# Tying modulation columns behind vector operations, ordering a feed-forward opening further by hand, and copying out one product

## The chip, the cores and the metric

One NeuronCore of a Trainium2 chip runs the whole program in one launch. The metric is the device time of an execution in microseconds (us); lower is better. Matrix products run on TensorE (PE in the profile), elementwise work on VectorE (DVE) and ScalarE (ACT), masks and a few accumulating transfers on GpSimd (POOL), and almost all transfers are issued from SyncE's queue (SP).

## The reference, cut to what matters

The kernel computes one layer of a transformer block for 512 tokens of width 1024 in float32, starting with six modulation vectors from a condition `c`:

```
mod = silu(c) @ w_ada + b_ada                  # 6 vectors of 1024
shift1, scale1, gate1, shift2, scale2, gate2 = split(mod, 6)
h = rmsnorm(x, g1) * (1 + scale1) + shift1
... = split(h @ w_in)                          # two branches' q, k, v, gates
merged = g_sb * (stick_breaking(...) @ w_proj_sb) + g_ret * (retention(...) @ w_proj_ret)
x = x + gate1 * (merged @ w_out)
h = rmsnorm(x, g2) * (1 + scale2) + shift2
a, u = split(h @ w_ffn_in)                     # 2 x 2816 columns
x = x + gate2 * ((silu(a) * u) @ w_ffn_out)
return rmsnorm(x, g_final)
```

Retention has four heads; each normalises its output and multiplies it by `silu(r_g)`.

## The kernel before, in words

Activations lie transposed, eight tiles of 128 features x 512 tokens. Each float32 operand is split into a high and a low part (ScalarE rounds the high part, VectorE subtracts it to give the low part, lines 205 and 207), and a product is three matmuls (line 226 in the profile, through `mm3`): high x high, high x low, low x high. Weights come as 512 KB blocks through three `raw` buffers into four `whi` and four `wlo` tiles. PSUM has eight banks: four named `ps`, three named `z`, one `av`.

Outside of stretches marked `manual_schedule` a planner sets the order of the instructions on every engine: it runs the program against its own model of costs, and takes, of what is ready there, what was written first. Inside such a stretch VectorE, ScalarE and TensorE keep the written order. `tc.issue_after(ins)` puts what is written under it behind `ins` on the engine of `ins`; transfers are not bound by it. Every engine executes its instructions in the fixed order, so one that waits holds all behind it.

**Modulation columns.** A 128-wide piece of `mod` is made on VectorE: a block of `w_ada` is multiplied by the broadcast `silu(c)` and summed along its row (line 254, one instruction and a small read of the sum), and the bias is added (line 257). `ada(n)` makes two such columns and loads two blocks (512 KB each) into the two `araw` buffers. n = 0 to 7 (shift1, scale1) are made in a hand-ordered start. n = 8 to 23 (gate1, shift2, scale2, gate2) are needed only from 740 us on; they are written at the end of each retention head, four per head, and the planner puts them where it sees room.

**Retention.** For each head `ret_scores` multiplies queries and keys (24 matmuls, tiles q), splits the scores (lines 205, 209) and masks them on GpSimd (line 599); `ret_out` multiplies by the values (tiles s, v); `ret_gate` makes four gate products of 24 matmuls, each ending in two multiplications and a split on VectorE (lines 789, 790, 207); then come the next head's queries, keys (rotated on VectorE, lines 680 to 682) and values (split, line 207, tile v); `ret_proj` makes eight projections (line 809 adds them up). The products of the next head begin while the last one's vector work goes on.

**Start.** While the first `x` tiles are squared and summed, `keep_busy(6)` gives TensorE six matmuls that no one reads.

**Feed-forward.** The input product for a pair of 256-column stripes p (11 of them) is a 2 x 2 block scheme of seven products (1 to 7) of sums of weight quarters with sums of activation quarters (S1 to S4, A11 and so on). In stripe p product 5 starts bank `v` and product 3 adds to it; between them the content after product 5 alone is used: line 1095 adds it to the sum u3 once product 7 is there, into the tile of `p1`. The weight sums t5, t6, t7, t4 are made on VectorE (line 1010), from quarters of which two lie in the `araw` buffers. Some low parts are made without VectorE: ScalarE writes the negated high part (line 969) and GpSimd issues a transfer that adds the raw weight onto it (line 970).

**The opening** (lines 1192 to 1302) is ordered by hand from the last output products to stripe 0's products 4, 6, 5, 7. Those are written with `late=True`: high x high and low x high first, and high weight x low activation in a second pass. After them the planner orders stripe 2's product 1, stripe 0's product 3, stripe 2's product 2 and stripe 1's product 6, their operands, and all that follows:

```
    queue = list(work)
    with tc.issue_after(held), tc.issue_after(held_act):
        del queue[:3]
        load_raws(1, [(0, 1), (1, 1)])
        sums(1, t5="s", t6="s", t7="h", t4="h")
```

Here `held` is the low part of S3 on VectorE and `held_act` its high part on ScalarE.

Of the kernel before, what the change touches and what calls it, by code (L numbers as in the profile page):

```python
# [113 lines left out]
def kernel(  # L114
# [9 lines left out]
    nc = tc.nc  # L124
# [78 lines left out]
    def split(dst_hi, dst_lo, src, scale=1.0, eng=None):  # L203

        nc.scalar.activation(dst_hi, src, AF.Copy, scale=scale)  # L205
        if isinstance(scale, float) and scale == 1.0:
            (eng or nc.vector).tensor_sub(dst_lo, src, f(dst_hi))  # L207
        else:
            nc.vector.scalar_tensor_tensor(  # L209
                dst_lo, src, scale, f(dst_hi), op0=ALU.mult, op1=ALU.subtract  # L210
            )
# [13 lines left out]
    def mm(o, lhs, rhs, start, stop):  # L225
        nc.tensor.matmul(o, lhs, rhs, start=start, stop=stop, skip_group_check=True)  # L226
# [208 lines left out]
    with tc.manual_schedule(engines={nc.vector.engine, nc.scalar.engine, nc.tensor.engine}):  # L435
# [23 lines left out]
        keep_busy(6)  # L459
# [320 lines left out]
    def ret_gate(h, os_, y):  # L780
        r = bcast(y, psa())
        ys = []
        for e in range(4):
# [8 lines left out]
            split(hl[:, 0, :], hl[:, 1, :], t)  # L792
            ys.append(hl)
        return ys
# [3 lines left out]
    def ret_proj(h, ys):  # L798
        for i in range(4):
            hi, lo = weight(("pr", h, i))  # L800
            for c in range(2):
# [3 lines left out]
                if p_ret[d] is None:  # L805
                    p_ret[d] = otile()
                    nc.vector.tensor_copy(p_ret[d], o)
                else:
                    nc.vector.tensor_add(p_ret[d], p_ret[d], o)
# [8 lines left out]

    qk = ret_qk(0, qk_ps)
    vt = ret_v(0, v_ps)  # L820
    gains2 = []
    for h in range(RH):
# [181 lines left out]
    def sums(p, **tags):  # L1004
        raw, t = raws_of[p], sums_of.setdefault(p, {})
        for key, tag in tags.items():
# [3 lines left out]
            nc.vector.tensor_sub(t[n], raw[a], t[b] if b in t else raw[b])  # L1010
# [34 lines left out]
    def product(p, n, o, first, last, at=None, then=None, late=False):  # L1045
# [3 lines left out]
        ah, al = acts7[SEVEN[n]]  # L1049
        for i in range(2):  # L1050
            c = slice(i * P, (i + 1) * P)
            for k in range(4):
# [4 lines left out]
                if late:  # L1057
                    mm(oc, hi[:, k, c], ah[:, k, :], a, False)
                    mm(oc, lo[:, k, c], ah[:, k, :], False, False)
                else:  # L1060
                    mm3(oc, hi[:, k, c], lo[:, k, c], ah[:, k, :], al[:, k, :], a, z)
        if late:
            for i in range(2):
                c = slice(i * P, (i + 1) * P)
                for k in range(4):
                    mm(o[:, i * 256 : (i + 1) * 256], hi[:, k, c], al[:, k, :],
                       False, last and i == 1 and k == 3)

    def run_product(p, n):

        d = part.setdefault(p, {})
        if n == 1:
            d["x"] = ps()
            product(p, 1, d["x"], True, False)
            d["p1"] = tmp()
            nc.scalar.activation(d["p1"], d["x"], AF.Copy)
        elif n == 2:
            product(p, 2, d["x"], False, True)
            d["s0"] = tmp()
            nc.scalar.activation(d["s0"], d["x"], AF.Silu)  # L1080
        elif n == 6:
            d["z"] = psz()
            product(p, 6, d["z"], True, True)
            d["u2"] = tmp()
            nc.vector.tensor_add(d["u2"], d["z"], d["p1"])
        elif n == 5:
            d["v"] = psz()
            product(p, 5, d["v"], True, False)
        elif n == 7:
            d["w"] = psz()  # L1090
            product(p, 7, d["w"], True, True)
            d["u3"] = tmp()
            nc.vector.tensor_add(d["u3"], d["w"], d["u2"])
            d["c22"] = d["p1"]
            nc.vector.tensor_add(d["c22"], d["v"], d["u3"])
        elif n == 4:
            d["y"] = ps()
            product(p, 4, d["y"], True, True)
            nc.vector.tensor_add(d["u3"], d["y"], d["u3"])
            nc.scalar.activation(d["u3"], d["u3"], AF.Silu)  # L1100
        else:
            assert n == 3
            product(p, 3, d["v"], False, True)
# [88 lines left out]
    with tc.manual_schedule(engines={nc.vector.engine, nc.scalar.engine, nc.tensor.engine}):  # L1192
# [89 lines left out]
        product(0, 4, d0["y"], True, True, late=True)  # L1282
# [3 lines left out]
        product(0, 6, d0["z"], True, True, late=True)  # L1286
# [4 lines left out]
        held_act = high7("S3", s3, "q")  # L1291
        ready[0, 7] = low(t0[7], k7, wtile("h"))
        held = low7("S3", s3, "q")
# [10 lines left out]
    queue = list(work)  # L1304
    with tc.issue_after(held), tc.issue_after(held_act):
        del queue[:3]
        load_raws(1, [(0, 1), (1, 1)])
        sums(1, t5="s", t6="s", t7="h", t4="h")
        load_raws(2, [(0, 1), (1, 1)])
# [4 lines left out]
    d0["u3"] = tmp()  # L1314
# [144 lines left out]
```

## Time and profile before

| what | value |
|---|---|
| time, median of 3 runs (range) | 1200.77 us (1200.19 to 1202.09) |
| the profiled execution: its own time | 1201.79 us |
| its span, first to last instruction | 1200.0 us |
| TensorE busy | 1173.0 us, 98% |
| VectorE busy | 831.2 us, 69% |
| ScalarE busy | 554.6 us, 46% |
| GpSimd busy | 32.4 us, 3% |
| granted TensorE clock, mean share | 0.995 |

The profiled execution's time is 1.79 us more than its span. The clock share is 1.0 where TensorE was granted its full 2.4 GHz and 0.5 where it was granted 1.2 GHz. Ends of matmuls are modelled, so that TensorE's busy time says little on its pace; idle time and the spacing of starts say more. Stages by time: start to 60 us, retention to about 500, stick-breaking attention to about 750, its projection and the output product to about 830, the opening of the feed-forward to about 875, and the feed-forward to the end.

### The profile page before, as it was taken

What the parts mean: (1) busy time and instruction counts of PE and PEld (TensorE: products, weight loads), DVE (VectorE), ACT (ScalarE), POOL (GpSimd) and SP (SyncE); (2) the same over time, 40 slices, a digit from 0 to 9 for tenths busy, and PEclk for the clock granted to TensorE, in tenths of its full rate; (3) what the DMA queues carried; (4) which work ended last, traced back from release to release, by engine and by line L of the source; (5) the groups of instructions that cost most, each with busy time, mean ns of one, the idle gap of its engine ahead of it and who ended that gap; (6) DMA issues with size and microseconds to landing.
All of it is one profiled execution on the core that took longest, in us unless ns stands there. A gap on an engine that the chain in (4) does not pass through costs nothing.

```text
span 1200.0 us, 16991 instructions
## 1 busy us (share of the span) xinstructions
PE 1173.0 (98%) x6707; PEld 1030.7 (86%) x6707; DVE 831.2 (69%) x1277; ACT 554.6 (46%) x823; POOL 32.4 (3%) x60
## 2 busy tenths in 40 slices
PE   7999899999999999999999999999999999999996
PEld 6988778888888888898889888889999999999996
DVE  7989885545554534377778787756888776767666
ACT  4443323323332332377677778344934544445432
POOL 0010000000000000000000000000100000000000
PEclk9999999999999999999999999999999999999999
DMA  9747771331333255435353635743445654565332
GB/s 351 267 140 229 242 256 59 91 95 47 94 117 88 68 141 152 142 92 127 103 136 98 152 83 161 245 110 86 109 154 163 180 161 112 158 176 158 88 89 71
DMA packets 53136, 167.72 MB, mean 140 GB/s; under 512 B 6592, under 2 KB 8768, under 8 KB 53056
## 3 DMA queue, kind: packets, MB, share of 16 engines
q1 hardware_dynamic: 49168, 154.04, 41.8%
q0 software_dynamic: 3312, 12.06, 5.5%
q8 instruction: 53, 0.87, 0.3%
q10 hardware_dynamic: 576, 0.52, 0.1%
q14 instruction: 27, 0.22, 0.1%
HBM read 135.67 MB, written 4.19 MB: 117 GB/s over the span
## 4 chain that ended last, share of the span: by engine, by line
PE 86%; DVE 6%; DMA 4%; ACT 2%; issue 2%; POOL 0%; SPq 0%; DVEq 0%; POOLq 0%; ACTq 0%
PE ps L226 62%; PE z L226 21%; PE av L226 3%; DMA araw<-wada 3%; DVE araw L254 1%; DVE wlo L207 1%; DMA h<-h 0%; DMA o<-xT 0%; ACT h L1209 0%; DMA t<-t 0%; DVE o L1134 0%; ACT t L626 0%; DVE t L473 0%; DVE s L209 0%; DVE t L682 0%
## 5 line engine op out<-in xcount | busy, mean ns | idle before, releaser
L226 PE MATMUL ps<-h,whi 128*128 128x512 f32 (+1 forms) x1410 | 416.0, 376 | 0.0
L226 PEld LDWEIGHTS ps<-h,whi 128*128 128x128 f32 x1410 | 256.2, 188 | 44.0
L205 ACT ACTIVATE whi<-raw 128x1024 fp32r<-128x1024 f32 (+1 forms) x138 | 144.3, 1046 | 280.1 <-PE ps L226 245.5
L226 PE MATMUL ps<-h,wlo 128*128 128x512 f32 (+1 forms) x705 | 262.6, 376 | 0.0
L207 DVE TENSOR_TENSOR wlo<-raw,whi 128x1024 fp32r<-128x1024 f32 (+1 forms) x138 | 166.3, 1205 | 92.4 <-ACT whi L205 55.7
L226 PEld LDWEIGHTS ps<-h,wlo 128*128 128x128 f32 x705 | 132.8, 188 | 23.2
L226 PE MATMUL ps<-s,whi 128*128 128x512 f32 x480 | 149.1, 392 | 2.6 <-DVE v L207 2.6
L226 PE MATMUL ps<-whi,h 128*128 128x256 f32 (+1 forms) x480 | 114.9, 326 | 1.4 <-DVE t L680 1.4
L226 PEld LDWEIGHTS ps<-s,whi 128*128 128x128 f32 x480 | 90.0, 190 | 21.1 <-DVE v L207 3.0
L226 PE MATMUL z<-q,whi 128*128 128x256 f32 x504 | 107.6, 283 | 0.0
L226 PE MATMUL ps<-s,wlo 128*128 128x512 f32 x240 | 93.8, 391 | 0.0
L207 DVE TENSOR_TENSOR s<-t,s 128x512 fp32r<-128x512 f32 (+1 forms) x122 | 77.0, 651 | 24.2 <-ACT s L205 24.0
L226 PEld LDWEIGHTS ps<-whi,h 128*128 128x128 f32 x480 | 82.3, 190 | 10.3 <-DVE t L680 2.3
L205 ACT ACTIVATE s<-t 128x512 fp32r<-128x512 f32 (+1 forms) x122 | 70.9, 599 | 36.6 <-DVE t L790 20.7
L226 PEld LDWEIGHTS z<-q,whi 128*128 128x128 f32 x504 | 85.4, 192 | 1.5
L226 PE MATMUL ps<-wlo,h 128*128 128x256 f32 (+1 forms) x240 | 78.0, 325 | 0.0
L925 DVE SCALAR_TENSOR_TENSOR o<-ps,mod,o 128x512 f32<-128x512 f32 (+1 forms) x63 | 42.4, 681 | 35.5 <-PE ps L226 35.5
L226 PEld LDWEIGHTS ps<-s,wlo 128*128 128x128 f32 x240 | 45.3, 189 | 9.6
L226 PEld LDWEIGHTS ps<-wlo,h 128*128 128x128 f32 x240 | 45.5, 190 | 4.0
L226 PE MATMUL ps<-q,whi 128*128 128x256 f32 (+1 forms) x224 | 48.9, 313 | 0.0
L226 PE MATMUL z<-qp,whi 128*128 128x256 f32 x168 | 47.3, 283 | 0.9 <-DVE t L1315 0.9
L226 PE MATMUL z<-q,wlo 128*128 128x256 f32 x168 | 47.5, 283 | 0.0
(268 smaller groups left out, 1835.9 us busy)
## 6 DMA issues: line engine op xcount, KB each, us to landing
raw<-wp SPq DMA_DIRECT2D x163, 512.0 KB, 3.7
araw<-wada SPq DMA_DIRECT2D x32, 512.0 KB, 4.4
araw<-wp SPq DMA_DIRECT2D x22, 512.0 KB, 5.0
sraw<-wada SPq DMA_DIRECT2D x16, 512.0 KB, 7.6
q<-qp SPq DMA_DIRECT2D x32, 256.0 KB, 3.7
o<-xT SPq DMA_DIRECT2D x16, 256.0 KB, 4.5
q<-qp SPq DMA_DIRECT2D x32, 128.0 KB, 3.6
s<-raw POOLq DMA_DIRECT2D x8, 512.0 KB, 7.1
```

The costliest lines, as they stand in the source:

```text
L205: nc.scalar.activation(dst_hi, src, AF.Copy, scale=scale)
L207: (eng or nc.vector).tensor_sub(dst_lo, src, f(dst_hi))
L226: nc.tensor.matmul(o, lhs, rhs, start=start, stop=stop, skip_group_check=True)
L254: nc.vector.scalar_tensor_tensor(raw, raw, 1.0, cact, op0=ALU.mult, op1=ALU.mult, accum_out=col)
L925: nc.vector.scalar_tensor_tensor(x1[d][:, hv], o[:, hv], mod[:, gcol + d : gcol + d + 1], x1[d][:, hv], op0=ALU.mult, op1=ALU.add,)
```

## The change

Sixteen calls of `ada` leave the ends of the heads and are made one at a time: each is bound behind one vector instruction, in each head behind the split of the second and the fourth gate product and behind the second and the fourth pair of projections. The transfers stay free. `keep_busy(6)` becomes `keep_busy(16)`. The hand-ordered opening goes on over stripe 2's product 1, stripe 0's product 3 and stripe 2's product 2, the last two of which take high x high and high weight x low activation first and the low weight last; the sums of stripe 1, its product 6's operands and the silu steps are written into that order too, and all later work of the three engines is bound behind the last vector, scalar and matrix instruction of it. After product 5 ScalarE copies bank `v` to a tile of its own (`c22`); the addition to u3 then reads that tile. `split`, `mm` and `sums` return their last instruction. The core of the diff:

```
-        keep_busy(6)
+        keep_busy(16)
@@ ret_gate
-            split(hl[:, 0, :], hl[:, 1, :], t)
+            ins = split(hl[:, 0, :], hl[:, 1, :], t)
             ys.append(hl)
+            if e % 2:
+                ada_after(ins)
@@ ret_proj
+                    ins = nc.vector.tensor_add(p_ret[d], p_ret[d], o)
+            if i % 2:
+                ada_after(ins)
@@ new
+    later = list(range(8, 24))
+    def ada_after(ins):
+        with tc.issue_after(ins.ins):
+            n = later.pop(0)
+            sh, sc = ada(n)
+            if 12 <= n < 20:
+                j = n - 12
+                gains2.append((gain(sc, sm[:, SM_G2 + j : SM_G2 + j + 1]), sh))
@@ after each head's ret_proj
-        ada(8 + h)
-        for j in (2 * h, 2 * h + 1):
-            sh, sc = ada(12 + j)
-            gains2.append((gain(sc, sm[:, SM_G2 + j : SM_G2 + j + 1]), sh))
-        ada(20 + h)
@@ product(..., late)
+        early = ((hi, ah), (lo, ah)) if late == "a" else ((hi, ah), (hi, al))
+        rest = (hi, al) if late == "a" else (lo, ah)
@@ take_out (was in run_product)
         elif n == 5:
+            d["c22"] = tmp()
+            nc.scalar.activation(d["c22"], d["v"], AF.Copy)
         elif n == 7:
             nc.vector.tensor_add(d["u3"], d["w"], d["u2"])
-            d["c22"] = d["p1"]
-            nc.vector.tensor_add(d["c22"], d["v"], d["u3"])
+            nc.vector.tensor_add(d["c22"], d["c22"], d["u3"])
@@ opening, after S4's high part and prepare(2, 2)
+        load_raws(1, [(0, 1), (1, 1)])
+        sums(1, t5="s")
-        product(0, 5, d0["v"], True, False, late=True)
-        product(0, 7, d0["w"], True, True, late=True)
+        product(0, 5, d0["v"], True, False, late="a")
+        product(0, 7, d0["w"], True, True, late="a")
         low7("S4", s4, "q")
+        sums(1, t6="s")
+        d0["c22"] = tmp()
+        nc.scalar.activation(d0["c22"], d0["v"], AF.Copy)
...
+        k6 = high(t1[6], wtile("whi"))
+        nc.scalar.activation(d0["u3"], d0["u3"], AF.Silu)
+        product(2, 1, d2["x"], True, False)
+        held_act = nc.scalar.activation(d2["p1"], d2["x"], AF.Copy).ins
+        ready[1, 6] = low(t1[6], k6, wtile("wlo"))
+        sums(1, t7="h")
+        product(0, 3, d0["v"], False, True, late="w")
+        held_pe = product(2, 2, d2["x"], False, True, late="w")
+        held = sums(1, t4="h")
@@ after it
+    def after_opening():
+        hold = ExitStack()
+        for ins in (held, held_act, held_pe):
+            hold.enter_context(tc.issue_after(ins))
+        return hold
+    with after_opening():
+        load_raws(2, [(0, 1), (1, 1)])
+        take_out(0, 3)
+        take_out(2, 2)
+        del queue[:4]
+    del work[:3]
+        with after_opening():
             (run_out if it[0] == "out" else run_product)(*it[-2:])
```

## Rows read from the trace of the kernel before

**Rows 1.** The profile's page: busy us (share) and instructions of each engine
```profile
PE 1173.0 (98%) x6707; PEld 1030.7 (86%) x6707; DVE 831.2 (69%) x1277; ACT 554.6 (46%) x823; POOL 32.4 (3%) x60
```

**Rows 2.** Waits of TensorE by releaser: total us, times, longest us
```profile
PE ps L226 <- DVE v L207: 2.6, 1, 2.6
...
PE ps L226 <- DMA h<-h: 1.7, 1, 1.7
...
PE ps L226 <- DVE t L680: 1.4, 1, 1.4
...
PE z L226 <- POOL s L599: 1.3, 2, 1.0
...
PE z L226 <- DVE s L209: 1.0, 1, 1.0
...
PE z L226 <- DVE t L1315: 0.9, 1, 0.9
```

**Rows 3.** Stretches: length, busy us (instructions) by engine, TensorE clock, DMA share, GB/s
```profile
30.00:60.00 30.00, 30.00 (x192) 27.10 (x191) 30.00 (x48) 14.67 (x25) 0.00 (x0) 1.00 0.75 267
...
150.27:153.68 3.41, 2.88 (x7) 2.30 (x8) 3.40 (x5) 0.00 (x0) 0.00 (x0) 0.50 0.84 303
...
200.00:500.00 300.00, 299.55 (x1417) 250.93 (x1416) 148.24 (x214) 91.68 (x118) 4.70 (x16) 1.00 0.35 103
...
875.00:1175.00 300.00, 300.00 (x2083) 281.31 (x2083) 215.60 (x246) 134.58 (x156) 13.56 (x16) 1.00 0.49 139
```

**Rows 4.** Timeline, VectorE near 150 us: start, us, what, [idle before <-releaser]
```profile
148.91 1.23 DVE L254 SCALAR_TENSOR_TENSOR araw<-araw,cact 128x1024 f32<-128x1024 f32 x1 [1.23 <-DMA araw<-wada]
...
150.06 2.48 DVE L207 TENSOR_TENSOR v<-ps,v 128x512 fp32r<-128x512 f32 x4
```

**Rows 5.** The column products' line: count, ns least/median/most, first and last start
```profile
L254 DVE SCALAR_TENSOR_TENSOR araw<-araw,cact x32: 1212/1222/1226, 51.9 to 174.2; 128x1024 f32<-128x1024 f32 x32
```

**Rows 6.** Waits of SyncE's DMA queue, whole span, on the column products
```profile
SPq L200 <- DVE araw L254: 40.8, 22, 5.5
```

**Rows 7.** Timeline of VectorE between head 2's projection and head 3's scores
```profile
378.70 0.69 DVE L809 TENSOR_TENSOR o<-o,ps 128x512 f32<-128x512 f32 x1 [2.03 <-PE ps L226]
...
379.57 1.22 DVE L207 TENSOR_TENSOR wlo<-raw,whi 128x1024 fp32r<-128x1024 f32 x1 [0.18 <-ACT whi L205]
...
380.71 0.48 DVE L209 SCALAR_TENSOR_TENSOR s<-z,con,s 128x256 fp32r<-128x256 f32 x1
```

**Rows 8.** Timeline of the feed-forward opening, 860 to 877 us, four engines
```profile
860.22 1.28 ACT L1313 ACT_TABLE_LOAD   x1
...
865.41 1.05 ACT L969 ACTIVATE h<-h 128x1024 fp32r<-128x1024 f32 x1
...
866.75 0.83 POOL L970 DMA_DIRECT2D h<-h  x1 [2.51 <-ACT h L969]
...
869.18 0.35 PE L226 MATMUL z<-qp,whi 128*128 128x256 f32 x1 [0.91 <-DVE t L1315]
...
871.74 1.45 PE L226 MATMUL ps<-v,h 128*128 128x256 f32 x10 [1.71 <-DMA h<-h]
...
876.14 1.23 DVE L1010 TENSOR_TENSOR h<-araw,araw 128x1024 f32<-128x1024 f32 x1 [3.04 <-DMA araw<-wp]
```

**Rows 9.** Groups, ScalarE, 840 to 1180 us: busy us, mean ns | idle
```profile
L1076 ACT ACTIVATE t<-ps 128x512 f32<-128x512 f32 x9 | 5.2, 577 | 0.0
```

**Rows 10.** Timeline of TensorE in the first 12 us
```profile
6.94 1.55 PE L226 MATMUL ps<-negones 128*128 128x512 f32 x6
...
11.34 2.86 PE L226 MATMUL z<-t,ones 128*128 128x256 f32 x12 [2.85 <-DVE t L473]
```

**Rows 11.** Timeline of GpSimd's masks (heads 0 and 1) and VectorE beside head 0's
```profile
68.16 5.38 POOL L599 TENSOR_SCALAR_AFFINE_SELECT s<-s 128x256 fp32r<-128x256 f32 x8 [66.68 <-DVE s L209]
...
178.40 2.41 POOL L599 TENSOR_SCALAR_AFFINE_SELECT s<-s 128x256 fp32r<-128x256 f32 x8 [104.85 <-DVE s L209]
...
72.18 1.21 DVE L254 SCALAR_TENSOR_TENSOR araw<-araw,cact 128x1024 f32<-128x1024 f32 x1
```

More of the change, by code (lines that the diff above doesn't have):

```diff
@@ L206, in split @@
         if isinstance(scale, float) and scale == 1.0:
[L207 to L211, printed above, removed]
+            return (eng or nc.vector).tensor_sub(dst_lo, src, f(dst_hi))
+        return nc.vector.scalar_tensor_tensor(
+            dst_lo, src, scale, f(dst_hi), op0=ALU.mult, op1=ALU.subtract
+        )
     def weight(key, eng=None):
@@ L1043, with product @@
     part = {}
-    def product(p, n, o, first, last, at=None, then=None, late=False):
+    def product(p, n, o, first, last, at=None, then=None, late=None):
         hi, lo = (tiles(t) for t in ready.pop((p, n)))
         ah, al = acts7[SEVEN[n]]
+        early = ((hi, ah), (lo, ah)) if late == "a" else ((hi, ah), (hi, al))
+        rest = (hi, al) if late == "a" else (lo, ah)
         for i in range(2):
@@ L1057, in product @@
                 if late:
-                    mm(oc, hi[:, k, c], ah[:, k, :], a, False)
-                    mm(oc, lo[:, k, c], ah[:, k, :], False, False)
+                    for n_, (w, x) in enumerate(early):
+                        mm(oc, w[:, k, c], x[:, k, :], a and n_ == 0, False)
                 else:
@@ L1062, in product @@
         if late:
+            w, x = rest
             for i in range(2):
@@ L1065, in product, with take_out @@
                 for k in range(4):
-                    mm(o[:, i * 256 : (i + 1) * 256], hi[:, k, c], al[:, k, :],
-                       False, last and i == 1 and k == 3)
+                    ins = mm(o[:, i * 256 : (i + 1) * 256], w[:, k, c], x[:, k, :],
+                             False, last and i == 1 and k == 3)
+            return ins
     def run_product(p, n):
         d = part.setdefault(p, {})
+        if n in (1, 4):
+            d["xy"[n > 1]] = ps()
+        elif n in (5, 6, 7):
+            d[" vzw"[n - 4]] = psz()
+        product(p, n, d[" xxvyvzw"[n]], n not in (2, 3), n not in (1, 5))
+        take_out(p, n)
+    def take_out(p, n):
+        d = part[p]
         if n == 1:
-            d["x"] = ps()
-            product(p, 1, d["x"], True, False)
             d["p1"] = tmp()
@@ L1281 @@
         nc.scalar.activation(d1["p1"], d1["x"], AF.Copy)
-        product(0, 4, d0["y"], True, True, late=True)
+        product(0, 4, d0["y"], True, True, late="a")
         d1["x2"] = ps()
@@ L1285 @@
         d0["z"], d0["v"], d0["w"] = psz(), psz(), psz()
-        product(0, 6, d0["z"], True, True, late=True)
+        product(0, 6, d0["z"], True, True, late="a")
         high7("S1", s1, "qp")
@@ L1290 @@
         low7("S1", s1, "q")
[L1291 removed]
+        high7("S3", s3, "q")
         ready[0, 7] = low(t0[7], k7, wtile("h"))
[L1293 removed]
+        low7("S3", s3, "q")
         d0["u2"] = tmp()
```

50 lines of the change are left out of this document (19 added, 31 removed).

## Prediction, made before the result was known

> **What bounds the kernel now.** I read the page first, then who TensorE waits for, then stretches, then timelines around each wait. TensorE is busy for 1173.0 of 1200.0 us [rows 1]. That share says nothing of pace, since ends are modelled; waits do. From 875 to 1175 us it is busy for all 300.00 us while VectorE has 84 us to spare [rows 3]: there only fewer or faster matmuls would help, and the change offers none. What can be had are TensorE's waits, and rows 2 names the ones that this change goes near: 2.6 us for a value split (tile v, line 207), 1.4 us for a rotation (line 680), 1.0 us for a score split (line 209), all three between 125 and 180 us, and in the feed-forward opening 1.7 us for a transfer into an h tile and 0.9 us for a sum on line 1315.
>
> The three in retention have one cause. All 32 column products run between 51.9 and 174.2 us [rows 5], that is in the first head and a half. VectorE runs in order; at 148.91 us a product sits idle for 1.23 us for its transfer, and the value splits queued behind it begin at 150.06 us [rows 4], while TensorE waits for the first of them to free a bank. A price comes on top: after that wait the granted clock is 0.50, or 1.2 GHz, from 150.27 to 153.68 us [rows 3].
>
> **The change part by part.** Durations and waits are of one profiled execution, whose own time is 1201.79 us: 1200.0 of span and 1.79 around it.
>
> *Columns, what goes.* Waits of 2.6, 1.4 and 1.0 us [rows 2]. The wait of 2.6 us ends at 150.8 us (0.7 us after the splits begin), so 2.88 us of work, the busy time in that stretch [rows 3], ran at half clock: 1.44 us lost. If the wait goes, I take the fall of the clock to go with it. Sum: 2.6 + 1.4 + 1.0 + 1.44 = 6.44 us. The 32 products cost 32 x 1.22 = 39 us of VectorE either way [rows 5]; in later heads they have cover, for TensorE is held by its own gate and projection gemms there.
>
> *Columns, what comes.* Sixteen ties, four a head; each puts two products behind its vector instruction, 2 x (1.22 + 0.08 for reading the sum) = 2.6 us at most. Behind the second and fourth gate product and the second projection pair, TensorE has further gemms that need none of the results, and I cost these at nothing. If that cover is missing, the bound is the one such wait shown: 1.4 us a tie. The fourth projection pair is different: the next thing is the scores of the next head, whose splits are late already. Ahead of head 3 the last addition starts at 378.70, a weight's low part at 379.57 and the first score split at 380.71 us [rows 7]. With the tie two products start at about 379.4 and end at about 381.7, where the score split is ready at 380.7: 1.0 us later. The weight's low part then falls behind. Three boundaries lead into scores (heads 1, 2, 3): 3 x 1.0 = 3.0 us, all on the path, since head 1's wait (1.0 us, counted as gone above) shows that this chain has no cover. Bounds: 0, if the planner lays the products behind the split, and 3 x 2.1 = 6.3 us, if the masks suffer too (second rival). I take 3.0, nearest to rows 7.
>
> *Their transfers.* SyncE's queue waits for an `araw` buffer 22 times, 40.8 us in all and 5.5 us at longest [rows 6], with weight loads behind. After the change the next pair is asked for as soon as the last is used, a tie early, and ties are at least 11 us apart (two gemms of 24 matmuls at some 0.23 us: six in rows 10 take 1.55 us with the tail of the last). The products should find their blocks landed; I cost this at nothing, with 5.5 us per event as the other end (last rival).
>
> *Opening.* Stripe 2's product 2 waits for its low part: ScalarE copies at 865.41, GpSimd issues at 866.75, and TensorE starts again at 871.74 us [rows 8], 5.0 us later. Two things help. The table load (1.28 us at 860.22 us) and two silus move behind this copy, so that the transfer is issued about 1.3 + 2 x 0.6 = 2.5 us earlier and lands near 869.3. And the low weight is now wanted last: from about 868 us (869.18 less the idle time) TensorE has product 3's 24 matmuls and 16 of product 2 before it, 40 at some 0.12 us (ten take 1.45 us with the tail of the last, rows 8), up to 872.8 us. It has some 3 us in hand. The wait on line 1315 goes because bank `v` is copied out before product 7 ends. Both waits: 0.91 + 1.71 = 2.6 us. Upper bound 2.9 us: idle time counts from modelled ends, 0.28 us behind a start, where the next start would come 0.12 us behind, so each wait hides 0.16 us more. Lower bound 0: what is late next is stripe 0's take-out, which the first output product needs 2.6 us sooner than before; a sum of stripe 2 that sat 3.04 us on a transfer (to 876.14 us, rows 8) could come ahead of it on VectorE and take all of that back. I take 2.6, because the take-out is written first.
>
> *The copy.* One ScalarE copy of 0.577 us [rows 9] in each of 11 stripes, 6.3 us, on an engine busy for 134.58 of 300 us [rows 3], beside products. VectorE has the same additions. Nothing; bounds 0 and, if each delayed a weight, 11 x 0.6 = 6 us, which the absence of any idle time on TensorE in that stretch speaks against.
>
> *keep_busy(16).* Six start at 6.94 us and TensorE next works at 11.34 us, after 2.85 us idle for VectorE [rows 10]. Ten more at 0.23 us end near 10.6 us, still 0.7 us ahead. Even if this lifted the clock of what follows, from 30 to 60 us VectorE is busy for 30.00 of 30.00 us [rows 3] and sets the pace. Nothing; bounds 0 and, were the clock half then, 3.0 us (16 x 0.46 = 7.4 us from 6.94, to 14.3 instead of 11.3).
>
> **Sum.** -6.44 + 3.0 - 2.6 = -6.0 us: 1195.8 us for an execution like the profiled one. The median lies 1.02 us under that execution, so I forecast 1194.8 us.
>
> **Rivals.** (a) *The boundary is hidden.* The planner puts the products after the score split, or fills TensorE with gate gemms. For: it is free to choose. Against: it takes what is written first among what is ready, and the columns are now written before the scores. Then -6.44 - 2.6 = -9.0: 1191.8 us.
>
> (b) *Masks stretch.* In head 0 the eight masks take 5.38 us where head 1's take 2.41, and a column product starts at 72.18 us in their midst [rows 11]; TensorE waits 1.3 us for them [rows 2]. Products or weight splits pushed into the masks add up to 1.0 us a mask. Each boundary then costs 2.1 and not 1.0 us: -6.44 + 6.3 - 2.6 = -2.7: 1198.1 us. Against: products bound behind the last addition are mostly over when masks begin. The Trainium skill (SBUF — State Buffer, Summary: rules for kernel authors) says that when VectorE reads two operands from SBUF and GpSimd reads SBUF as well, whichever comes second is blocked until the first is done. By that rule the weight's low part, moved into the masks, would do the same harm as a column product; the difference of 2.97 us in rows 11 agrees.
>
> (c) *The opening gives nothing*, because the take-out or a late sum takes over the wait: -6.44 + 3.0 = -3.4: 1197.4 us.
>
> (d) *Slower.* The ties put 2.6 us of products ahead of a bank's release where TensorE has none in hand. The place: the tie behind each fourth gate product, followed by the next head's rotations, and the boundary. Price: 3 x 1.4 for rotations, 6.3 for boundaries, and 5.5 us for one column pair that is not landed and holds a weight load in SyncE's queue: 16.0 us, less 6.44 + 2.6: +7.0, 1207.8 us; without the queue's 5.5 it is +1.5. It decides from the point where VectorE is more than one gemm (5.5 us) behind or a weight comes later than its three buffers cover. Against: heads 2 and 3 leave VectorE half idle (148 of 300 us busy from 200 to 500 us, rows 3).
>
> (e) *No effect of the ties*, the planner making the columns as early and as tightly as before: only -2.6, 1198.2 us. Against: head 3 begins at 380 us [rows 7], and order behind its instructions is binding.
>
> **How the numbers follow.** Chances: forecast 0.53, (a) 0.15, (b) 0.10, (c) 0.10, (d) 0.09, (e) 0.03. About 0.2%, 2.4 us, is what a measurement can tell from no change: faster means under 1198.4 us. Faster: all of the forecast but 0.03, (a), half each of (b) and (e), and 0.06 of (c): 0.77. Slower: 0.07 of (d), and 0.04 for a transfer or clock that comes out against both parts: 0.11. The rest, 0.12, is the same. The range goes from 1190.5 us, (a) with the opening's upper bound (0.3 more) and a us of scatter (the runs before lie 0.6 below to 1.3 above their median), to 1200.6 us, (b) and (c) together: 6.44 - 6.3 = 0.1 under 1200.8. It leaves out most of (d) and a tail below.
>
> **What would show it.** Column products should start behind ties, beyond 90 us and on past 400 us; TensorE's waits for v and line 680 and the half clock near 150 us gone; at the three boundaries the first score split starts about 3 us behind the start of the last addition instead of 2.0 (rows 7), with waits of about 1 us each; no wait longer than 0.3 us from 867 to 885 us, and the first output product 3 us closer to the opening. The forecast is wrong if column products wait for transfers at their ties, if TensorE waits for rotations, if masks stretch to over a us, or if the 300 us behind the opening show idle time.

## The result, and the profile after

| kernel | median us (range, runs) | ratio to before [95% interval] |
|---|---|---|
| before | 1202.09 (1200.19 to 1206.71, 5) | |
| after | 1192.13 (1191.97 to 1193.24, 5) | 0.9916 [0.9893, 0.9938] |

The forecast was 1194.8 us, the range 1190.5 to 1200.6 us. The profiled execution of after took 1191.98 us, its span is 1190.3 us: 9.7 us under before's 1200.0, where 6.0 were forecast.

The page's line of engines (columns as in [rows 1]) cannot show this. TensorE's busy time is the same 1173.0 us, and ten of its instructions more are the ten idle matmuls of the start.

```profile
PE 1173.0 (99%) x6717; PEld 1031.6 (87%) x6717; DVE 829.6 (70%) x1277; ACT 560.1 (47%) x834; POOL 33.2 (3%) x60
```

The waits of TensorE do (total, times, longest). All that stood in [rows 2] are gone but one: masks on GpSimd, 1.3 us in two waits before, are 2.3 us in four. No wait on line 207 (tile v), line 680, line 209, on an h transfer or on a sum in the opening is left.

```profile
PE z L225 <- DVE mod L446: 4.0, 1, 4.0
PE z L225 <- POOL s L598: 2.3, 4, 1.1
PE av L225 <- DVE diag L338: 0.9, 4, 0.3
PE z L225 <- DVE t L1213: 0.8, 1, 0.8
PE ps L225 <- ACT h L427: 0.2, 1, 0.2
```

(After's lines 225, 253, 208, 598, 810, 978, 979 and 1324 are before's 226, 254, 209, 599, 809, 969, 970 and 1315.) The next view is by stretch, columns as in [rows 3]. From 14 to 24 us the mean clock is 1.00. From 200 to 500 us VectorE now has 174.16 us of work where it had 148.24, and TensorE 298.95 where it had 299.55: that is where the columns went and what their ties cost there. Behind the opening TensorE is busy throughout, as in [rows 3].

```profile
14.00:24.00 10.00, 9.86 (x52) 8.18 (x51) 9.73 (x18) 5.37 (x12) 0.00 (x0) 1.00 1.03 405
...
200.00:500.00 300.00, 298.95 (x1411) 250.16 (x1411) 174.16 (x290) 91.27 (x118) 6.45 (x16) 1.00 0.48 145
870.00:1165.00 295.00, 295.00 (x2041) 276.30 (x2040) 212.40 (x242) 136.30 (x162) 13.56 (x16) 1.00 0.50 140
```

The column products' line (against [rows 5]) and the waits of SyncE's queue on them (against [rows 6]): the same 32 at the same 1.22 us, spread from 95.1 to 466.2 us instead of 51.9 to 174.2. The queue waits longer in sum (55.7 against 40.8 us) and nobody minds: VectorE has no idle time ahead of a product, where before it had 8.7 us.

```profile
L253 DVE SCALAR_TENSOR_TENSOR araw<-araw,cact x32: 1215/1220/1224, 95.1 to 466.2; 128x1024 f32<-128x1024 f32 x32
```

```profile
SPq L200 <- DVE araw L253: 55.7, 15, 4.8
```

A time per stage follows from the same events in both traces (first start, us):

| event | before | after | gained since the last |
|---|---|---|---|
| head 0's scores | 64.86 | 64.96 | -0.10 |
| head 0's column sums, behind its masks | 82.55 | 80.95 | 1.70 |
| head 1's scores | 174.02 | 167.17 | 5.25 |
| head 2's scores | 276.78 | 269.96 | -0.03 |
| head 3's scores | 378.50 | 372.28 | -0.60 |
| first scores of the stick-breaking branch | 513.58 | 507.82 | -0.46 |
| stripe 0's product 5, in the opening | 859.24 | 852.72 | 0.76 |
| last matmul | 1190.79 | 1181.05 | 3.22 |

The gains add up to 9.74 us. The second and the third row need one correction between them: three gate matmuls of 0.23 us each that stood ahead of head 0's column sums stand behind them in after, so that 0.68 us of the 1.70 belong to the row below. Like for like, head 0's masks give 1.02 us and the way to head 1's scores 5.93; the other rows hold the same matmuls in both kernels. TensorE at head 0's masks, before and then after (start, duration, what, [idle before <- releaser]):

```profile
70.75 2.56 PE L226 MATMUL z<-s,v 128*128 128x256 f32 x15 [1.00 <-POOL s L599]
73.60 5.46 PE L226 MATMUL z<-s,v 128*128 128x512 f32 x30 [0.29 <-POOL s L599]
```

```profile
70.84 7.75 PE L225 MATMUL z<-s,v 128*128 128x256 f32 x45 [0.58 <-POOL s L598]
```

The next timelines show two more of these places. At the boundary before head 3 on VectorE (start, duration, what, [idle before <- releaser]; compare [rows 7]) the two products stand behind the last addition, the first score split starts 2.96 us behind that addition's start instead of 2.01, and the weight's low part, which stood ahead of the split, falls in among the masks:

```profile
372.48 0.69 DVE L810 TENSOR_TENSOR o<-o,ps 128x512 f32<-128x512 f32 x1 [2.03 <-PE ps L225]
373.08 1.22 DVE L253 SCALAR_TENSOR_TENSOR araw<-araw,cact 128x1024 f32<-128x1024 f32 x1
...
374.23 1.22 DVE L253 SCALAR_TENSOR_TENSOR araw<-araw,cact 128x1024 f32<-128x1024 f32 x1
...
375.44 0.47 DVE L208 SCALAR_TENSOR_TENSOR s<-z,con,s 128x256 fp32r<-128x256 f32 x1
...
377.73 1.22 DVE L207 TENSOR_TENSOR wlo<-raw,whi 128x1024 fp32r<-128x1024 f32 x1
```

GpSimd's masks (compare [rows 11]): head 0's take 2.78 + 0.54 us instead of 5.38, head 3's 3.36; heads 1 and 2 are like head 3. Of head 3's eight masks one takes 1.21 us, beginning at 377.89 us beside the low part at 377.73; the others take 0.29 to 0.41 us.

```profile
68.25 2.78 POOL L598 TENSOR_SCALAR_AFFINE_SELECT s<-s 128x256 fp32r<-128x256 f32 x6 [66.78 <-DVE s L208]
71.49 0.54 POOL L598 TENSOR_SCALAR_AFFINE_SELECT s<-s 128x128 fp32r<-128x128 f32 x2 [0.46 <-DVE s L208]
...
375.99 3.36 POOL L598 TENSOR_SCALAR_AFFINE_SELECT s<-s 128x256 fp32r<-128x256 f32 x8 [98.96 <-DVE mod L256]
```

In the opening (timelines of ScalarE, GpSimd and TensorE; compare [rows 8]) ScalarE copies product 2's weight at 856.71 us, ahead of the table load, and GpSimd issues the transfer at 858.06 us. Stripe 2's product 1 starts at 858.48 us: the issue is 0.42 us ahead of it. Before, the issue came at 866.75 us [rows 8], 1.75 us behind that product's start at 865.00 us, so against the products it comes 2.2 us earlier. Product 3, with its low weight in the last eight, and product 2 follow without a gap. The transfer itself takes longer than before, though: 6.2 us from issue to landing (last view: KB, us to landing), where it took 4.9, so that it lands at 864.25 us. Against product 1 that is 0.9 us earlier than before, for an issue 2.2 us earlier.

```profile
856.71 1.06 ACT L978 ACTIVATE h<-h 128x1024 fp32r<-128x1024 f32 x1
857.67 0.58 ACT L1318 ACTIVATE t<-z 128x512 f32<-128x512 f32 x1
858.27 1.28 ACT L1322 ACT_TABLE_LOAD   x1
...
858.06 0.83 POOL L979 DMA_DIRECT2D h<-h  x1 [2.14 <-ACT h L978]
...
858.48 3.04 PE L225 MATMUL ps<-v,s 128*128 128x256 f32 x24
861.36 2.08 PE L225 MATMUL z<-q,whi 128*128 128x256 f32 x16
863.28 1.12 PE L225 MATMUL z<-q,wlo 128*128 128x256 f32 x8
864.24 3.04 PE L225 MATMUL ps<-v,h 128*128 128x256 f32 x24
```

```profile
h<-h POOLq DMA_DIRECT2D x1, 512.0 KB, 6.2
```

### The profile page after: what moved, and what is told of

Read it like the earlier page. It is cut to its first block, busy times and chain, and to the rows that moved or that the text cites. A ratio compares the mean times of both kernels' runs of the same rounds, so it can differ in the third digit from the quotient of the medians.

```text
span 1190.3 us, 16997 instructions
## 1 busy us (share of the span) xinstructions
PE 1173.0 (99%) x6717; PEld 1031.6 (87%) x6717; DVE 829.6 (70%) x1277; ACT 560.1 (47%) x834; POOL 33.2 (3%) x60
## 4 chain that ended last, share of the span: by engine, by line
PE 90%; issue 6%; DVE 3%; POOL 1%; ACT 0%; DVEq 0%; ACTq 0%; POOLq 0%
PE ps L225 68%; PE z L225 19%; PE av L225 3%; POOL s L598 1%; DVE araw L253 1%; DVE s L208 0%; DVE o L1145 0%; ACT t L625 0%; DVE o L810 0%; DVE t L1213 0%; DVE diag L338 0%; ACT t L626 0%; ACT t L319 0%; DVE t L321 0%; DVE t L322 0%
```

## The experiments

**Each part alone**, four kernels on one chip, where before took 1203.17 us (1200.52 to 1207.90, 25 runs).

Columns alone: the 16 ties and nothing else.

```
-        ada(8 + h)        # and three more pairs at the end of each head
+            if e % 2:     # in ret_gate
+                ada_after(ins)
+            if i % 2:     # in ret_proj
+                ada_after(ins)
```

> The kernel before with the sixteen ties alone. Theory A (the gain is the sum of single TensorE waits): 1.5 us in head 0's masks, 4.1 us for the value split and the rotation, 1.4 us for the half clock near 150 us, less some 1.1 us at the borders of heads 2 and 3: about 6 us less than before, with the waits in the opening left at about 2.6 us. Theory B (the extra matmuls at the start and the clock bring a part): under 4.5 us here. The planner could also lose what the ties gain elsewhere: then the scores of head 1 would not start about 6.8 us earlier than before.

Measured 1196.25 us (1195.41 to 1197.03, 5 runs), ratio 0.9939 [0.9919, 0.9959]. In its waits those of retention are gone, the masks are as in after, and the opening's two are there:

```profile
PE z L225 <- POOL s L598: 2.3, 4, 1.1
PE ps L225 <- DMA h<-h: 1.7, 1, 1.7
...
PE z L225 <- DVE t L1323: 0.9, 1, 0.9
```

Head 0's scores start at 64.29 and head 1's at 166.55 us: 102.26 us for a head that took 109.16 before, by ties alone. At the opening's second wait the clock falls in this execution, which before's profiled one did not show there (a stretch, columns as in [rows 3]). It costs 1.4 us: from product 5 to the last matmul this execution takes 332.97 us, and before's, with the same two waits, 331.55.

```profile
865.08:868.50 3.42, 3.33 (x15) 3.33 (x16) 1.50 (x3) 0.63 (x1) 0.00 (x0) 0.50 0.99 320
```

Opening alone: the hand-ordered opening with its three holds, and the copy of bank `v` in every stripe, as in the whole change; columns and start as before.

```
...
+        product(0, 3, d0["v"], False, True, late="w")
+        held_pe = product(2, 2, d2["x"], False, True, late="w")
+        held = sums(1, t4="h")
...
```

> The kernel before with the opening ordered further and product 5 copied out, columns and start as before. Theory A: the opening's wait is independent of the columns: 3.2 us less than before, no wait of TensorE from the opening's start to the first output product, head stage unchanged. Rival: column traffic and opening interact (the quarter loads sit in the same two buffers), then the gain here is clearly under or over 3.2 us, and the sum with the run of ties alone misses the whole change by more than 1.5 us.

Measured 1198.59 us (1195.92 to 1200.44, 8 runs), ratio 0.9958 [0.9942, 0.9975]. The opening's waits are gone and retention's are there, with other lengths than in [rows 2]:

```profile
PE ps L225 <- DVE t L679: 1.8, 1, 1.8
PE z L225 <- DVE s L208: 1.5, 1, 1.5
PE ps L225 <- DVE v L207: 1.5, 1, 1.5
```

So both parts are worth something by themselves, and the intervals allow them to add up to the whole: 0.9939 x 0.9958 = 0.9897 against 0.9916 [0.9893, 0.9938]. The traces show that they do: from product 5 to the last matmul open_only takes 328.33 us, the same as after, and the rows of head 0 to head 3 take the same time in cols_only as in after, within 0.05 us each.

Start alone, and copy alone:

```
-        keep_busy(6)
+        keep_busy(16)
```

> The kernel before with sixteen idle matmuls at the start instead of six. Theory A: the half clock from 17 to 20.6 us goes or not, but the first scores start at 64.9 us as before, since VectorE sets the pace there: within 0.5 us of before. Theory B: without the half clock the start is 1.7 us shorter, and the time with it.

```
+            d["c22"] = tmp()
+            nc.scalar.activation(d["c22"], d["v"], AF.Copy)
-            d["c22"] = d["p1"]
-            nc.vector.tensor_add(d["c22"], d["v"], d["u3"])
+            nc.vector.tensor_add(d["c22"], d["c22"], d["u3"])
```

> The kernel before with the copy of product 5 alone (ScalarE copies bank v to a tile of its own in all stripes, the addition reads the tile). Theory A: the steady feed-forward has no TensorE wait to win or lose, so within 1 us of before; the wait on the sum behind product 7 in the opening (0.9 us) may go, but the wait for the low part's transfer takes its place. Rival C (the copy is what frees the opening): at least 1.5 us less than before.

Measured 1204.14 us (1200.89 to 1207.17, 12 runs), ratio 1.0004 [0.9991, 1.0017], and 1201.97 us (1198.36 to 1206.90, 12 runs), ratio 0.9996 [0.9979, 1.0014]: neither can be told from no change. Copy alone leaves the opening's own addition as it was, so it says nothing on the copy there; both of the opening's waits stay. None of the nine profiles with sixteen idle matmuls has half clock in the start (stretch of start alone, clock 1.00; before's mean from 14 to 24 us is 0.83), and of the five with six, cols_only and all_busy6 have none either. Head 0's scores start no earlier for it (65.07 against 64.86 us).

```profile
14.00:24.00 10.00, 9.85 (x52) 8.14 (x51) 9.62 (x18) 5.47 (x13) 0.00 (x0) 1.00 1.03 406
128.71:132.12 3.41, 3.35 (x8) 2.67 (x9) 3.41 (x6) 0.63 (x1) 0.00 (x0) 0.50 0.66 245
```

The second line is half clock at another place, at the end of a wait of 2.1 us on line 680. The profiled execution of copy alone, its slowest (1206.90 us), has five such stretches ahead of the tail: two before 22 us, and the three below. The first and the third come with waits that the change removes, the second with a wait of 1.8 us for ScalarE that it does not touch:

```profile
131.15:134.56 3.41, 3.41 (x9) 2.64 (x8) 3.41 (x8) 0.63 (x1) 0.00 (x0) 0.50 0.67 250
581.71:585.12 3.41, 3.41 (x16) 3.41 (x16) 1.67 (x3) 1.27 (x3) 0.00 (x0) 0.50 0.86 229
875.25:878.66 3.41, 3.29 (x15) 3.29 (x16) 1.53 (x3) 0.63 (x1) 0.00 (x0) 0.50 0.98 322
```

Each can cost up to 1.7 us (half of 3.41); the one at 875.25 us costs what cols_only's does, 332.97 us from product 5 to the last matmul. Kernels that keep retention's waits scatter over 4.5 to 8.5 us, those without them over 0.7 to 3.3 (in fewer executions). The granted clock of every execution is on record, and in the former it goes with the time: of before's 25 executions here, the 16 up to 1203.5 us have a mean clock of 0.995 to 0.997, the nine above 0.991 to 0.994. That the waits set the falls off is read from where the stretches begin; no run shows it by itself.

**What the pieces of the whole are worth**, four kernels on a second chip, where before took 1204.42 us (1199.74 to 1206.22, 9 runs). First the whole change with `keep_busy(6)`:

> The whole change, but six idle matmuls at the start. Theory A: within 0.5 us of the whole change (9 to 10 us less than before), whether or not a half-clock stretch comes back near 17 us. Theory B: 1.5 us or more slower than the whole change, with a half-clock stretch before 24 us.

Measured 1191.98 us (1191.80 to 1192.51, 4 runs), ratio 0.9897 [0.9880, 0.9915]: the same as after. The longer start is not needed, and this trace has no half clock ahead of the tail even with six. (On this chip that is 12.4 us less than before, not the 9 to 10 expected.)

Then the place of the projection's ties, moved one projection pair earlier, so that a pair of gemms stands between the last tie and the next head's scores:

```
-            if i % 2:
+            if i % 2 == 0:
                 ada_after(ins)
```

> The whole change with the projections' two ties behind the first and the third pair instead of the second and the fourth, so that no column product stands between the last addition and the next head's scores. Theory A (products behind the last addition delay the first score split by about 1 us and push a weight's low part into the masks): the first score split starts 2.0 us after the last addition again, no mask over 0.45 us in heads 1 to 3, and TensorE's waits for masks fall from 2.3 to under 1.2 us: 1 to 1.6 us less than the whole change. Rival (the borders cost nothing that the ties cause): within 0.5 us of the whole change.

Measured 1190.11 us (1189.15 to 1190.74, 4 runs), ratio 0.9880 [0.9862, 0.9898]: the best of all, 1.9 us under the kernel above (a little more than the 1 to 1.6 expected), on the same chip, and their ranges do not meet; the two also differ by the ten idle matmuls. VectorE at the boundary before head 3 is as it was before the change [rows 7], the low part ahead of the split, which starts 2.01 us behind the last addition:

```profile
370.71 0.69 DVE L810 TENSOR_TENSOR o<-o,ps 128x512 f32<-128x512 f32 x1 [0.52 <-PE ps L225]
371.58 1.23 DVE L207 TENSOR_TENSOR wlo<-raw,whi 128x1024 fp32r<-128x1024 f32 x1 [0.18 <-ACT whi L205]
372.72 0.48 DVE L208 SCALAR_TENSOR_TENSOR s<-z,con,s 128x256 fp32r<-128x256 f32 x1
```

and the one wait on masks that is left (0.6 us) is head 0's. Between scores, heads 1 to 3 take 101.89, 101.90 and 135.10 us here, and 102.79, 102.32 and 135.54 in after: 0.90 + 0.42 + 0.44 = 1.8 us, the price of the three boundary ties.

Third, a pair of products tied into the masks instead (behind the last score split, in place of the fourth projection tie):

```
+            ins = split(hl[:, 0, c : c + w], hl[:, 1, c : c + w], z[bank][:, c : c + w],
+                        gk[:, h * 4 + j : h * 4 + j + 1])
+        ada_after(ins)
...
-            if i % 2:
+            if i == 1:
```

> The whole change with each head's fourth tie moved behind the last score split of a head (heads 0 to 3), so that two column products run beside the last masks. Theory A (a vector instruction with two operands in SBUF holds a mask up for its length): two or three masks of each head take 1.2 us or more instead of 0.29, and TensorE waits about 1 us or more a head for them: 1 to 5 us slower than the same kernel with the early ties, though no score split is delayed. Rival (only the delay of the splits costs, masks stretch by chance): masks at 0.29 us, and the time within 0.5 us of the kernel with the early ties.

Measured 1196.54 us (1196.13 to 1197.79, 5 runs), ratio 0.9937 [0.9919, 0.9955]. VectorE, then GpSimd, at head 3: six masks take 0.76 + 1.03 us, and the last two, beside the products, 2.44:

```profile
380.70 1.22 DVE L253 SCALAR_TENSOR_TENSOR araw<-araw,cact 128x1024 f32<-128x1024 f32 x1
...
381.84 1.30 DVE L253 SCALAR_TENSOR_TENSOR araw<-araw,cact 128x1024 f32<-128x1024 f32 x1
```

```profile
377.99 0.76 POOL L598 TENSOR_SCALAR_AFFINE_SELECT s<-s 128x256 fp32r<-128x256 f32 x2 [98.27 <-DVE s L208]
379.28 1.03 POOL L598 TENSOR_SCALAR_AFFINE_SELECT s<-s 128x128 fp32r<-128x128 f32 x4 [0.53 <-DVE s L208]
380.85 2.44 POOL L598 TENSOR_SCALAR_AFFINE_SELECT s<-s 128x128 fp32r<-128x128 f32 x2 [0.54 <-DVE s L208]
```

The last two took 1.21 and 1.27 us one by one; others of their size go four in 1.03 us. TensorE waits for masks eight times, 5.0 us in all, and the kernel is 6.4 us slower than with the early ties, more than the 1 to 5 expected. All fourteen traces say the same: 54 masks started while a weight's low part or a column product was running on VectorE, and each took 1.21 to 1.35 us and ended 0.15 us behind that instruction; 42 masks in whose time such an instruction only began took 0.29 to 0.30 us. So a mask is held up for about as long as one VectorE instruction that reads two operands from SBUF, and not by the score splits, whose first operand is in PSUM (line 208 runs beside the four). The Trainium skill (SBUF — State Buffer, Summary: rules for kernel authors) says just this: the second of the two is blocked until the first has finished; these rows agree.

**The opening**, where two edits could each have removed the wait for the h transfer. Products 3 and 2 with the low weight in its usual place:

```
-        product(0, 3, d0["v"], False, True, late="w")
-        held_pe = product(2, 2, d2["x"], False, True, late="w")
+        product(0, 3, d0["v"], False, True)
+        held_pe = product(2, 2, d2["x"], False, True)
```

> The whole change, but products 3 and 2 of the opening take their low weight in the usual place instead of last. Theory A (the transfer is issued 2.3 us earlier because the table load and the silus stand behind it, and that alone is enough): no wait in the opening, within 0.5 us of the whole change. Rival (the low weight last is what removes the wait): 1 to 2 us of waiting on the transfer come back.

Measured 1193.06 us (1191.30 to 1194.41, 4 runs), ratio 0.9905 [0.9885, 0.9924]. The trace has no wait in the opening, and its last matmul starts at 1180.99 us (1180.98 in the whole change on this chip, with six idle matmuls). But the margin is thin: the transfer lands at 864.21 us, and product 2's first matmul on the low weight starts at 864.42. And the median is 1.1 us above that kernel's, more than the 0.5 expected.

Next, on a third chip (before 1202.03 us, 1199.51 to 1207.77, 9 runs), the table load and two silus put back ahead of the weight's copy, once without and once with the late low weight:

```
+        d1["s0"] = tmp()
+        nc.vector.tensor_add(d1["s0"], d1["x2"], d1["p1"])
+        for d in (d0, d1):
+            nc.scalar.activation(d["s0"], d["s0"], AF.Silu)
         prepare(2, 2)
...
-        d1["s0"] = tmp()      # the same four lines, behind c22's copy
```

> The whole change, but in the opening the table load, d1's first sum and the two silus stand before product 2's weight is copied (as in the kernel before), and products 3 and 2 take the low weight in the usual place. Theory A (what took the opening's wait away is that ScalarE copies this weight before the table load and the silus, so that GpSimd issues the transfer some 2.5 us earlier): the transfer of 'h' is issued at about 860.5 us instead of 858.06, and product 2 waits again for 1 to 1.7 us; the last matmul comes 1 to 1.7 us after 1181.0 us. Rival B (the wait went because the rest of the opening is laid out by hand, and the place of the silus is indifferent): no wait over 0.3 us in the opening, and the last matmul within 0.3 us of 1181.0.

> The whole change, but in the opening the table load, d1's first sum and the two silus stand before product 2's weight is copied; the order with the low weight last stays. The low weight is then wanted about 1.9 us later (16 matmuls at some 0.12 us) than in the usual place. Theory A: the transfer is issued about 2.5 us later than in the changed kernel and the late low weight covers most of it: a wait of 0 to 0.5 us, so that either half of this edit would have done alone and each is the reserve of the other. Rival C (the order with the low weight last brings nothing even then): the same wait as with the usual order, 1 to 1.7 us.

Measured 1193.08 us (1192.25 to 1194.04, 5 runs), ratio 0.9927 [0.9902, 0.9952], without, and 1191.43 us (1191.17 to 1192.02, 5 runs), ratio 0.9911 [0.9883, 0.9939], with it; the ranges do not meet. Without it the issue (GpSimd's timeline) falls 2.1 us behind product 1's start at 858.50 us, product 2 waits again, TensorE resumes 4.92 us behind the issue, and the last matmul starts at 1182.14 us, as theory A said:

```profile
860.55 0.84 POOL L979 DMA_DIRECT2D h<-h  x1 [4.60 <-ACT h L978]
```

```profile
864.26 0.40 PE L225 MATMUL ps<-v,h 128*128 128x256 f32 x2
865.47 2.90 PE L225 MATMUL ps<-v,h 128*128 128x256 f32 x22 [0.81 <-DMA h<-h]
```

With it, the transfer is issued as late (859.97 us, product 1 at 857.92) and no wait shows: the low weight is wanted only at 863.68 + 16 x 0.12 = 865.6 us, and lands at 864.90. So rivals B and C fall, and the two edits are each other's reserve; in these executions either does alone, the low weight last with 0.7 us in hand and the early issue with 0.2.

Last, open_no_late's four runs had come in two pairs 2.5 us apart, so I ran it and after once more together (fourth chip, before 1202.44 us, 1199.87 to 1205.32, 11 runs).

> The whole change with products 3 and 2 of the opening taking the low weight in the usual place, run again beside the changed kernel: the first time two of its four executions took 1191.3 and 1191.9 us and two took 1194.2 and 1194.4 us, while the profiled one had no wait in the opening. Theory A1 (the low weight last is a reserve for executions in which the transfer lands late, since the usual order leaves it only some 1.2 us in hand and the late one 3.1): the executions fall apart again, about half of them 2 us or more above the changed kernel's. Rival A2 (chance of those four): the same median as the changed kernel within 0.5 us, and the same scatter.

> The changed kernel once more, on the same chip. By both theories 1191.8 to 1193.3 us, as before; by theory A1 none of its executions is above 1193.5 us.

Measured 1193.10 us (1191.35 to 1194.69, 5 runs), ratio 0.9917 [0.9900, 0.9933], and 1192.66 us (1192.10 to 1194.81, 6 runs), ratio 0.9919 [0.9902, 0.9936]. The changed kernel has two executions above 1194.5 us itself, which A1 ruled out: A1 falls as it stood, and the scatter is there with the late low weight too. By the landings in these two profiles the low weight had 0.2 us in hand in the usual order and 1.8 us as the last, not the 1.2 and 3.1 expected. What the scatter comes from stays open (the five executions without it lie 3.3 us apart at one and the same mean clock, 0.998). The usual order has the higher median both times, by 1.1 and 0.4 us; a small worth of the late low weight is neither shown nor excluded.

## Why the prediction was right, and where it missed

Right in the sign, in the two places that pay, and in the range; 2.7 us too high against the median. The time measured is almost that of rival (a), 1191.8 us, but by chance: what (a) needs, products behind the score split, did not happen. By the steps of its sum, from the two traces (the shift of the three gate matmuls taken out):

| step | forecast us | measured us |
|---|---|---|
| value split, rotation, half clock near 150 us | -5.44 | -5.93 |
| score split of head 1, and the tie at that boundary | -1.0 + 1.0 | +0.03 |
| ties at the boundaries of heads 2 and 3 | +2.0 | +1.06 |
| head 0's masks | 0 | -1.02 |
| start | 0 | +0.10 |
| opening | -2.6 | -3.22 |
| stick-breaking branch to the opening | 0 | -0.76 |
| sum | -6.0 | -9.74 |

*Columns, what goes.* The mechanism held: no product is idle for a transfer, the splits are on time, and none of the ten profiles of kernels with ties shows half clock near 150 us. That the clock's fall would go with the wait was assumed and came out, but the size of this step is that of one execution: of the four profiles without ties only before's has half clock near 150 us (two have it near 130 us, one nowhere in retention), and from head 0's column sums to head 1's scores they take 89.4 to 91.5 us, the ten with ties 86.2 to 86.6. The products found their blocks landed, and no rotation waits: rival (d) did not happen, nor (e).

*Missed: head 0's masks.* The prediction had the row that prices it, masks of 5.38 us with a product in their midst [rows 11] and TensorE's 1.3 us for them [rows 2], but used it only against the change, in rival (b), as a thing that ties could do to heads 1 to 3. That ties also take the products out of head 0 never entered the sum. Nor was the product alone: of the three masks of head 0 that took over a us, one (72.21 us) started beside it and two (69.11 and 71.03) beside a weight's low part. In after the first of the three is left (1.34 us), the other two are gone, and with them TensorE's second wait of 0.29 us. The rest of the 1.02 us is mostly TensorE's order: two more gate matmuls now run ahead of the first wait, which ends as far behind the scores' start as before (5.9 us).

*Columns, what comes.* The delay of the split was foreseen to 0.05 us (2.96 us behind the addition). Its price was not: 1.0 us was put on the path at each boundary. TensorE lost 1.2 us at head 1, where it had lost 1.2 before, and 0.5 at the other two. And what it waits for is not the split but a mask, held up by the weight's low part that the products pushed back. So rival (b) named the right mechanism and the wrong size: one mask of eight is stretched by 0.9 us, and at heads 2 and 3 about half of that reaches TensorE. The prediction's own sign against itself, masks of over a us, came true without the time that it stood for. Head 1 pays more because there the low part gets in ahead of the last score split as well (VectorE's timeline at head 1), where at head 3 all the splits are through:

```profile
171.76 1.22 DVE L207 TENSOR_TENSOR wlo<-raw,whi 128x1024 fp32r<-128x1024 f32 x1
172.89 0.75 DVE L208 SCALAR_TENSOR_TENSOR s<-z,con,s 128x512 fp32r<-128x512 f32 x1
```

The sum read head 1's lack of cover into all three. With ties one pair earlier the whole term is 1.8 us less, so rival (a)'s result was to be had by another place for the tie, not from the planner.

*Opening.* Both waits went. The sum took 2.6 us from the waits as printed; from start to start TensorE lost 1.07 + 1.87 + 3 x 0.1 = 3.24 us there before, all of which came back (3.22). The prediction had bounded this at 2.9 us, and missed the 0.3 us of small gaps of the broken-up products. Rival (c) did not happen: no stretch behind the opening shows idle time. The 3 us in hand were 1.9: the low weight is wanted at 864.24 + 16 x 0.12 = 866.2 us, but the transfer lands at 864.25, for it takes 6.2 us and not the 5.0 that the sum carried over from before. With the usual order 0.2 us is left: of the two helps that the prediction added together, the runs show that each suffices, and that the early issue does so barely.

The reason given for the other wait is not borne out. Line 1315 adds product 7's bank `w` to u2 and does not read `v`; line 1317 does, and starts at 870.09 us, after the wait has ended. What kept TensorE waiting was VectorE's order. Before, the addition stood behind two weight sums and started 3.35 us behind product 1; in after (line 1324) it stands ahead of them and starts 1.10 us behind it:

```profile
868.35 0.68 DVE L1315 TENSOR_TENSOR t<-z,t 128x512 f32<-128x512 f32 x1
```

```profile
859.58 0.68 DVE L1324 TENSOR_TENSOR t<-z,t 128x512 f32<-128x512 f32 x1
```

No run takes the copy out of the opening and leaves the order, so that what the copy does there was not tested.

*Copy in the other stripes, and start.* Both nothing, as forecast. The step on the start had the ten matmuls end at 10.6 us; they take 0.26 us each and run until 11.55 us, when the next product starts (11.34 before). It cost nothing all the same, for the cover named there: VectorE sets the pace up to head 0.

*What no step had.* 0.76 us between retention and the opening: before's execution lost 1.04 us at 578.8 us behind ScalarE's line 205, at the end of a chain that begins with a transfer (tile t), and after's did not. It is there in other executions of changed kernels too (1.15 us at 571.0 us with the early ties, 0.75 us at 573.1 us in after's own second profile), so it is scatter and not the change.

The medians differ a little more than the traces (9.96 against 9.74 us), and the ratios of the other chips reach 0.9897 for the same kernel with six idle matmuls. The parts alone gained more by their medians (6.9 and 4.6 us) than the table of events gives them (1.02 + 5.93 - 0.03 - 0.60 - 0.46 = 5.86 for retention, 3.22 for the opening), within their intervals. Falls of the clock behind the waits that go, of which before's profiled execution had one on the path, would explain that; it is not shown.

## What to carry to other kernels

Work that is not urgent is best bound to a place where the engine that waits for its results, here TensorE, has gemms in hand, and not to the last instruction ahead of a chain that is already late: the same sixteen ties, with those of the projections one pair earlier, were worth 1.9 us more. When an instruction is pushed back, ask what the next one in its queue will now run beside; here TensorE waited not for the delayed split but for the mask that the weight's low part held up. An earlier issue is not as much of an earlier landing: measure the landing itself. A row that tells what a collision costs counts on both sides: for what the change may bring about, and for what it takes away.

## What the runs showed of the hardware that was not expected

A mask of 128 columns on GpSimd takes 0.29 us by itself. Started while a VectorE instruction with two operands in SBUF is running (1.21 to 1.30 us), it takes 1.21 to 1.35 us, and in all 54 cases it ended 0.15 us behind that instruction: it is held up as a whole, and does not share. What counts is which started first: the 42 masks that had begun 0.17 to 0.27 us ahead of such an instruction took 0.29 to 0.30 us.

Half clock of 3.41 us shows up at the end of or just behind single waits of 1.8 to 2.6 us, and at two of 0.9 and 1.7 us that follow each other, in some executions and not in others (the two waits: with it in cols_only and copy_only, without it in before and busy16_only; a wait of 1.8 us without it in open_only). One such stretch in the opening cost 1.4 us on top of its waits, and a kernel with several such waits has a time that scatters by 0.4 to 0.7%.

The accumulating transfer of 512 KB for product 2 took 4.8 to 4.9 us to land when it was issued 1.7 to 2.1 us behind product 1's start, and 6.2 to 6.3 us when it was issued 0.4 us ahead of it (eight profiles of kernels with the hand-ordered opening). What slows the early one was not shown.
